# Expert 0's tokens gathered by one-hot products instead of through HBM, with second-layer biases moved ahead of the experts

## The chip, the cores and the metric

One core of a Trainium2 chip runs the whole kernel. The time is device microseconds of one execution; lower is better. All times of the trace are in microseconds from the start of the span of one profiled execution.

## The reference

One transformer block on 512 tokens of width 1024, in f32: adaptive norm, an attention mixer (sparse and block attention together, output projection `w_out`), a second norm, and a mixture of 32 experts of which each token takes 4. The part that matters here:

```python
x = x + g1 * hybrid_mixer(h, ...)                       # h @ w_out at its end
h = rms_norm(x, ln2_g) * (1.0 + sc2) + sh2
logits = h @ router_w + router_b                        # 512 x 32
top_val, top_idx = lax.top_k(logits, 4);  gate = softmax(top_val)
u = h[toks] @ w1[e] + b1[e]                             # toks: the tokens that chose e
g_, lin = u[:, :1024], u[:, 1024:]                      # clamped
y = ((lin + 1) * g_ * sigmoid(1.702 * g_)) @ w2[e] + b2[e]
x = x + g2 * segment_sum(y * gate)
```

The weights of the experts, 32 times 12.6 MB, are most of what is read.

## The kernel before

**Products.** An f32 operand is split into a high part (cast to f32r on ScalarE) and a low part (subtraction on VectorE), and a product is made of three f32r products (high-high, high-low, low-high). Each 1 MB chunk of weights, 128x2048, comes by one DMA of SyncE into one of 7 raw buffers; `high(i)` (line 770) casts it on ScalarE and `low(i)` (line 774) subtracts on VectorE, three chunks ahead of their use. The split chunks go to the pools `wq` and, from the third chunk on, `wq2`, which is opened over the memory of the closed pool `op`.

**Projection and router.** The four tiles of 128 tokens pass through `project` (lines 88 to 90 by `mm3`), four chunks of w_out each, 12 products a chunk. After the last chunk of a tile, its `tail` is cut into four steps, of which one is called behind each chunk of the next tile; those of tile 3 run at the end without products between them. `turn`: the product is added to x (`xm`, line 838), `xm` is transposed (842) and its squares summed (845), a power on GpSimd gives the norm's factor (122). `logits`: the products with the router's weights (855). `gates`: the choice of the four largest on VectorE (863 to 871), their softmax (872 to 878), the normalised rows `xs` and the gates stored to the DRAM table `h2d` (874, 879). `counts`: `xm` stored to the output (882), and five small bf16 products (899) which count, for every token and expert, the tokens ahead of it.

**Slots.** From the counts each token has a place `pos_e` in each expert, and a token that didn't choose the expert got a place behind those that did. For an expert, `slots` (1027) makes one-hot rows from the places, `lookup` (1033) turns them into token numbers by a product, and `fetch` (1036, 1002) writes them as integers and gathers these rows of `h2d` by an indirect DMA into `xg`. `none` pushes the numbers of unused slots out of range. The gather of an expert comes two experts ahead; those of experts 0 and 1 follow the router directly.

**Experts.** Each expert has 12 steps, one weight chunk each: 8 of the first layer (`pu`, 1161) and, of the expert before, 4 of the second (`py`, 1185). Into the steps are put: the transposes of the activations (`pat`, 985, in steps 1 and 2), those of the next expert's rows (`pxt`, 1009, in steps 4 and 6) with their affine part (1016) and split (1045, 1049) into `XT`, the slots, lookup and fetch two experts ahead (steps 4, 7, 9), and at step 0 `emit`: the result times gate, scattered into the output by a DMA that adds (991, 993). In experts 1 to 4 the second-layer biases of one tile are made from its gates by a transpose (787) and two products (797) and added to the output by a further DMA that adds (799).

**Order.** `in_order` ties the instructions of TensorE, VectorE and ScalarE, each engine by itself, to the order in which the code issues them, from the projection to the last expert; the DMA issues of ScalarE are among them. GpSimd and SyncE are ordered by the scheduler. A tile of a pool with two buffers may be written when the last use of the tile two before it is over, DMAs included.

Of the kernel before, what the change touches and what calls it, by code (L numbers as in the profile page):

```python
# [48 lines left out]
def block_kernel(ctx, tc, x, c, ada_w, ada_b, ln1_g, ln2_g, w_in, nsa_q_gain, nsa_k_gain, nsa_cmp_pos,  # L49
# [48 lines left out]
    G.iota(piota, pattern=[[0, 1]], base=0, channel_multiplier=1, allow_small_or_imprecise_dtypes=True)  # L98
    siota = cst.tile([P, P], F32, name="siota")
    G.iota(siota, pattern=[[1, P]], base=0, channel_multiplier=0, allow_small_or_imprecise_dtypes=True)  # L100
# [622 lines left out]
    mask = mp.tile([P, NT, NE], BF, name="mask")  # L723
    pos_e = mp.tile([P, NT, NE], F32, name="pos_e")
    tokc = mp.tile([P, NT], F16, name="tokc")
    gatef = mp.tile([P, NT, NE], F32, name="gatef")
# [5 lines left out]

    none = mp.tile([P, NE], F32, name="none")
# [44 lines left out]
    def add_b2(t, pool):  # L778

        gh = mp.tile([P, P], F32R, tag="gh", name="gh")  # L780
        gT = mp.tile([P, P], F32R, tag="gT", name="gT")

        def gates():
            pg = psm.tile([P, P], F32, tag="ps", name="pgT")
            g4 = pool.tile([P, 4, NE], F32, tag="g4", name="g4", bufs=1)
            G.tensor_copy(g4, gatef[:, t, None, :].to_broadcast([P, 4, NE]))
            T.transpose(pg, g4.rearrange("p q e -> p (q e)"), ident)
            A.copy(gh, pg)
            A.copy(gT[0:64], pg[0:64])
            V.tensor_sub(gT[64:128], pg[64:128], gh[64:128].bitcast(F32))  # L790

        def add():
            ys = pool.tile([P, D], F32, tag="ysb", name="ysb", bufs=1)
            for h in range(2):
                hs = slice(512 * h, 512 * h + 512)
                pb = psm.tile([P, 512], F32, tag="ps", name="pb2")
                T.matmul(pb, gT, b2s[:, hs], start=True, stop=True)
                A.copy(ys[:, hs], pb)
            G.dma_start(out_rows[P * t:P * t + P, :], ys, accum_op=ALU.add)

        return gates, add

    with ExitStack() as oc:
# [4 lines left out]
        onesf = op1.tile([P, NE], F32, name="onesf")  # L808
        V.memset(onesf, 1.0)
        for t in range(NT):  # L810
            V.tensor_scalar(tokc[:, t:t + 1], piota, float(P * t), None, op0=ALU.add)

        onesb = op1.tile([P, P], BF, name="onesb")
        onesn = op1.tile([P, P], BF, name="onesn")
        trib = op1.tile([P, P], BF, name="trib")
        trin = op1.tile([P, P], BF, name="trin")
        tri2 = op1.tile([P, P], BF, name="tri2")
        tileb = op1.tile([P, NT, NE], BF, name="tileb")
        V.memset(onesb, 1.0)
        V.memset(onesn, -1.0)  # L820
        for w, m in ((trib, 1.0), (trin, -1.0), (tri2, 2.0)):
            V.tensor_scalar(w, siota, piota, m, op0=ALU.is_gt, op1=ALU.mult)
        for t in range(NT):
            V.memset(tileb[:, t], float(t))

        def tail(t, ps):

            st = op.tile([P, 4], F32, tag="st2", name="st2")
            xm = op.tile([P, D], F32, tag="xm", name="xm")
            xs = op.tile([P, D], F32, tag="xs", name="xs")  # L830
            hT = op.tile([P, KD, P], F32, tag="h2T", name="h2T", bufs=1)
            lg = op.tile([P, NE + 4], F32, tag="lg", name="lg")
            g = {}

            def turn():
# [3 lines left out]
                for h in range(2):  # L839
                    pt = psc.tile([P, 4, P], F32, tag="ps", name="ph2")  # L840
                    for k in range(4):
                        T.transpose(pt[:, k, :], xm[:, 128 * (4 * h + k):128 * (4 * h + k) + 128], ident)
                    if h == 0:
                        A.copy(hT[:, 0:4, :], pt)
                        A.activation(xs, xm, AF.Square, accum_out=st[:, 0:1])
                    else:
                        V.tensor_copy(hT[:, 4:8, :], pt)
# [80 lines left out]
        for t in range(2):  # L928
            load_x(t)
# [378 lines left out]
```

## Time and profile before

| | us |
|---|---|
| median of 3 runs (lowest to highest) | 1578.86 (1577.48 to 1579.42) |
| the profiled execution | 1579.63 |
| its span, first to last instruction | 1577.9 |
| TensorE busy | 1514.2 (96%) |
| VectorE busy | 1335.3 (85%) |
| ScalarE busy | 1100.5 (70%) |
| GpSimd busy | 344.3 (22%) |

The profiled execution is 0.8 us above the median. Engines in the rows: PE is TensorE's products, PEld its weight loads (they overlap the products), DVE VectorE, ACT ScalarE, POOL GpSimd, SP SyncE; a q behind the name is the engine's queue issuing a DMA. L1161 is line 1161. A matmul's duration overlaps the next one's, so the pitch of a stream is read from starts. [...] What stands in brackets behind an instruction is the time that its engine was idle before it, and what ended it.

### The profile page before, as it was taken

What the parts mean: (1) busy time and instruction counts of PE and PEld (TensorE: products, weight loads), DVE (VectorE), ACT (ScalarE), POOL (GpSimd) and SP (SyncE); (2) the same over time, 40 slices, a digit from 0 to 9 for tenths busy, and PEclk for the clock granted to TensorE, in tenths of its full rate; (3) what the DMA queues carried; (4) which work ended last, traced back from release to release, by engine and by line L of the source; (5) the groups of instructions that cost most, each with busy time, mean ns of one, the idle gap of its engine ahead of it and who ended that gap; (6) DMA issues with size and microseconds to landing.
All of it is one profiled execution on the core that took longest, in us unless ns stands there. A gap on an engine that the chain in (4) does not pass through costs nothing.

```text
span 1577.9 us, 20500 instructions
## 1 busy us (share of the span) xinstructions
PE 1514.2 (96%) x7533; PEld 1199.3 (76%) x7533; DVE 1335.3 (85%) x1533; ACT 1100.5 (70%) x1275; POOL 344.3 (22%) x258
## 2 busy tenths in 40 slices
PE   7998999999699999999999999999999999999996
PEld 5887745457578888888888888888888888888884
DVE  4779488653689999999999999999999999999994
ACT  4332366642688887788887777778888777778872
POOL 2216445410112112111112112211111212211110
PEclk9999999999799999999999999999999999999998
DMA  9755123035699999999999999999999999999991
GB/s 327 250 203 161 55 59 106 15 120 205 265 329 356 378 368 390 371 371 373 365 372 361 371 355 370 367 367 365 369 363 371 362 361 369 379 367 364 367 366 35
DMA packets 114879, 476.04 MB, mean 302 GB/s; under 512 B 15632, under 2 KB 27984, under 8 KB 82008
## 3 DMA queue, kind: packets, MB, share of 16 engines
q1 hardware_dynamic: 102680, 449.19, 75.8%
q0 software_dynamic: 9792, 19.17, 5.3%
q10 hardware_dynamic: 2304, 6.36, 1.1%
q8 instruction: 60, 0.98, 0.2%
q14 instruction: 43, 0.35, 0.1%
HBM read 468.55 MB, written 23.13 MB: 312 GB/s over the span
## 4 chain that ended last, share of the span: by engine, by line
PE 82%; issue 6%; DMA 6%; DVE 3%; ACT 2%; POOL 1%; SPq 0%; ACTq 0%; POOLq 0%; DVEq 0%
PE pu L1161 41%; PE py L1185 19%; DMA out_dram<-ys,idx 2%; PE po L657 2%; PE pz L88 2%; PE pz L90 2%; PE pz L89 2%; PE pu L1142 2%; PE pxt L1009 2%; DMA ada<-in_ada_w_dram 2%; PE pat L985 2%; PE ps L220 2%; PE pp L636 2%; DVE am L175 1%; PE pw L89 1%
## 5 line engine op out<-in xcount | busy, mean ns | idle before, releaser
L774 DVE TENSOR_TENSOR wlo<-w,whi 128x2048 fp32r<-128x2048 f32 x384 | 868.4, 2288 | 76.7 <-ACT whi L770 76.3
L770 ACT CAST whi<-w 128x2048 fp32r<-128x2048 f32 x384 | 732.7, 1910 | 213.9 <-PE pu L1161 144.5
L1161 PE MATMUL pu<-whi,XT 128*128 128x512 f32 x2048 | 526.6, 399 | 1.4 <-ACT XT L1045 1.4
L1161 PEld LDWEIGHTS pu<-whi,XT 128*128 128x128 f32 x2048 | 374.2, 189 | 75.0 <-ACT XT L1045 1.8
L1161 PE MATMUL pu<-wlo,XT 128*128 128x512 f32 x1024 | 275.4, 391 | 0.0
L1161 PEld LDWEIGHTS pu<-wlo,XT 128*128 128x128 f32 x1024 | 192.6, 188 | 42.1
L993 POOL DMA_INDIRECT out_dram<-ys,idx x32 | 157.8, 4932 | 287.8 <-DVE ys L991 250.8
L1002 POOL DMA_INDIRECT xg<-h2d,idx x32 | 44.9, 1402 | 597.5 <-PE py L1185 537.9
L1185 PE MATMUL py<-whi,ahi 128*128 128x512 f32 x508 | 136.6, 391 | 1.0 <-DVE ys L991 0.9
L1185 PE MATMUL py<-whi,alo 128*128 128x512 f32 x508 | 135.8, 389 | 0.0
L1185 PE MATMUL py<-wlo,ahi 128*128 128x512 f32 x508 | 135.8, 389 | 0.0
L1185 PEld LDWEIGHTS py<-whi,ahi 128*128 128x128 f32 x508 | 95.0, 188 | 21.4 <-ACT ahi L1110 1.1
L1185 PEld LDWEIGHTS py<-whi,alo 128*128 128x128 f32 x508 | 95.4, 188 | 19.9
L1185 PEld LDWEIGHTS py<-wlo,ahi 128*128 128x128 f32 x508 | 95.4, 188 | 19.9
L1016 ACT ACTIVATE xf<-pxt,colv 128x128 f32<-128x128 f32 x256 | 95.9, 456 | 6.9 <-PE pxt L1009 6.9
L88 PE MATMUL pz<-whi,hhi 128*128 128x512 f32 (+2 forms) x224 | 80.9, 364 | 4.6 <-ACT hsq L422 3.6
L89 PE MATMUL pz<-wlo,hhi 128*128 128x512 f32 (+2 forms) x224 | 78.3, 352 | 0.0
L90 PE MATMUL pz<-whi,hlo 128*128 128x512 f32 (+2 forms) x224 | 77.1, 353 | 0.0
L227 ACT ACTIVATE pr<-sb,sm 128x256 f32<-128x256 f32 (+3 forms) x93 | 51.7, 557 | 24.4 <-DVE sm L224 20.7
L175 DVE SCALAR_TENSOR_TENSOR am<-ada,cond,am 128x256 f32<-128x256 f32 x128 | 61.5, 518 | 1.3 <-DMA ada<-in_ada_w_dram 0.8
L82 ACT CAST whi<-win 128x1024 fp32r<-128x1024 f32 (+3 forms) x28 | 24.2, 871 | 46.7 <-PE pz L89 21.3
L224 DVE CUSTOM_DVE_ANT_0 sb<-ps,dtile 128x128 f32<-128x128 f32 (+3 forms) x96 | 44.2, 483 | 13.9 <-PE ps L220 10.4
(287 smaller groups left out, 1617.8 us busy)
## 6 DMA issues: line engine op xcount, KB each, us to landing
w<-in_exp_w_dram SPq DMA_DIRECT2D x384, 1024.0 KB
ada<-in_ada_w_dram SPq DMA_DIRECT2D x22, 1024.0 KB
win<-in_w_in_dram SPq DMA_DIRECT2D x6, 1024.0 KB
win<-in_w_in_dram SPq DMA_DIRECT2D x3, 768.0 KB
x<-in_x_dram SPq DMA_DIRECT2D x4, 512.0 KB
ada<-in_ada_w_dram SPq DMA_DIRECT2D x4, 512.0 KB
wo<-in_w_out_dram SPq DMA_DIRECT2D x4, 512.0 KB
wo<-in_w_out_dram SPq DMA_DIRECT2D x2, 1024.0 KB
```

What stands on the lines that cost most here:

```text
L88: T.matmul(o, lhi, rhi, start=start, stop=False, **kw)
L89: T.matmul(o, lhi, rlo, start=False, stop=False, **kw)
L90: T.matmul(o, llo, rhi, start=False, stop=stop, **kw)
L175: V.scalar_tensor_tensor(am[:, p:p + MOD_W], rr[k // 4][:, c0:c0 + MOD_W], cond[:, k:k + 1], am[:, p:p + MOD_W], op0=ALU.mult, op1=ALU.add)
L227: A.activation(tl[i], sb[:, :n], AF.Exp, scale=-1.0, bias=sm[:, 0, i:i + 1], accum_out=sm[:, 1, i:i + 1])
L770: A.copy(hi, raws[i])
L774: V.tensor_sub(lo, raws.pop(i), hi.bitcast(F32))
L993: G.indirect_dma_start(out=out_rows, out_offset=bass.IndirectOffsetOnAxis(ap=icol, axis=0), in_=ys, in_offset=None, compute_op=ALU.add, bo ...
L1002: G.indirect_dma_start(out=xg, out_offset=None, in_=h2d, in_offset=bass.IndirectOffsetOnAxis(ap=icol, axis=0), bounds_check=S - 1, oob_is_ ...
L1016: A.activation(dst[:, j, :], pt[:, j, :], AF.Identity, scale=colv[:, 0, k:k + 1], bias=colv[:, 1, k:k + 1])
L1161: T.matmul(pu[h][g], XT[:, x, c, :], w[:, c0:c0 + 512], start=False, stop=last)
L1185: T.matmul(py[n], prev.a[k // 4][x][:, k % 4, :], w[:, cs], start=(k == 0 and x == 0 and w is hi), stop=(k == KD - 1 and w is lo))
```

## The change

- Expert 0 isn't gathered through `h2d`. One-hot rows of its places (`oh0`, f32, 128x128 a tile) are made behind each tile's choice, and 32 f32 products of 128x128x128 (`gather0`) add its rows up, already transposed, in two PSUM banks (`px`). The rows of all four tiles stay on chip (`rows_of`). Those of tiles 0 to 2 and the start of expert 0's bias products (`pu_start`) are issued during and after the tail of tile 3; then affine (shared by ScalarE and VectorE) and split into `XT0`. Its gates and token numbers come from an f32 lookup at step 1 of expert 0.
- Places start at 1, and a token that didn't choose an expert has place 0, so only its own tokens fill slots. `none` goes, as do three of the five counting products, their tables and the product that prepared them. Token numbers are held less 512, so that an unused slot gives 512, which is out of range.
- The second-layer bias of a tile is added to `xm` on VectorE before `xm` is stored to the output. It is called two steps after the next tile's `turn` (tile 2's between `turn` and `logits` of tile 3; tile 3's last).
- The tail's steps: `choose`, `rows`, `store`, `gates`, `place` in place of `gates` and `counts`. A chunk of tile 1 is projected before the last of tile 0, and the steps start one chunk later. x has one buffer, loaded after the tile before has been used. The squares are summed by halves.
- In each expert both transposes of the activations stand in step 1, and both of the next expert's rows in step 5 behind the lookup (then affine in steps 5 and 7, low parts in 6 and 8); slots in step 3, fetch in 7. The lookup's PSUM comes from `psc`. Expert 1's lookup and fetch stand in step 1 of expert 0, its slots before the loop. Chunk 1 is split within the end of the tail, chunk 2 after it.

The core of the diff (of lines that only moved, most are left out):

```diff
-    def add_b2(t, pool):
-        ...
-            G.dma_start(out_rows[P * t:P * t + P, :], ys, accum_op=ALU.add)
+    def affine(dst, pt, h, js=range(4)):
+        for j in js:
+            k = 4 * h + j
+            A.activation(dst[:, j, :], pt[:, j, :], AF.Identity, scale=colv[:, 0, k:k + 1], bias=colv[:, 1, k:k + 1])
+    def pu_start(e):
+        sel = [bsel[:, v, e:e + 1].to_broadcast([P, P]) for v in range(2)]
+        pu = [[psz.tile([P, 512], F32, tag="ps", name="pu") for _ in range(2)] for _ in range(2)]
+        for h in range(2):
+            for g in range(2):
+                T.matmul(pu[h][g], *bias(1024 * g + 512 * h, sel), start=True, stop=False)
+        return pu
...
+        def add_b2(t, xm):
+            gh = op1.tile([P, P], F32R, tag="gh", name="gh")
+            gT = op1.tile([P, P], F32R, tag="gT", name="gT")
+            g4 = op1.tile([P, 4, NE], F32, tag="g4", name="g4")
+            def turn():
+                G.tensor_copy(g4, gatef[:, t, None, :].to_broadcast([P, 4, NE]))
+                pg = psc.tile([P, P], F32, tag="ps", name="pgT")
+                T.transpose(pg, g4.rearrange("p q e -> p (q e)"), ident)
+                A.copy(gh, pg)
+                A.copy(gT[0:64], pg[0:64])
+                V.tensor_sub(gT[64:128], pg[64:128], gh[64:128].bitcast(F32))
+            def add():
+                for h in range(2):
+                    hs = slice(512 * h, 512 * h + 512)
+                    pb = psc.tile([P, 512], F32, tag="ps", name="pb2")
+                    T.matmul(pb, gT, b2s[:, hs], start=True, stop=True)
+                    V.tensor_add(xm[:, hs], xm[:, hs], pb)
+                nc.scalar.dma_start(out_rows[P * t:P * t + P, :], xm)
+            return turn, add
+        rows_of = [op1.tile([P, D], F32, name=f"xs{t}") for t in range(NT)]
+        def gather0(t, h, ks=range(4)):
+            for k in ks:
+                T.matmul(px[h][:, k, :], rows_of[t][:, 512 * h + P * k:512 * h + P * k + P], oh0[:, t, :], start=t == 0 and k == 0,
+                         stop=t == NT - 1 and k == 3, skip_group_check=True)
         def tail(t, ps):
             xm = op.tile([P, D], F32, tag="xm", name="xm")
-            xs = op.tile([P, D], F32, tag="xs", name="xs")
+            xs = rows_of[t]
...
+            def place():
                 m = mask[:, t, None, :]
-                count(pp[:, 0:2 + t], onesb, m.to_broadcast([P, 2 + t, NE]))
-                ...
+                T.matmul(pd[:, t], trib, mask[:, t], start=t == 0, stop=True, skip_group_check=True)
+                V.scalar_tensor_tensor(pos_e[:, t], pd[:, t], 1.0, mask[:, t], op0=ALU.add, op1=ALU.mult)
+                V.tensor_scalar(oh0[:, t], siota, pos_e[:, t, 0:1], None, op0=ALU.is_equal)
+                T.matmul(pd[:, t + 1:], onesb, m.to_broadcast([P, NT - t, NE]), start=False, stop=True,
+                         skip_group_check=True)
...
+        for t, c in [(0, 0), (0, 1), (0, 2), (1, 0), (0, 3)] + [(1, c) for c in (1, 2, 3)] + \
+                [(t, c) for t in (2, 3) for c in range(4)]:
+            if t not in ps:
+                ps[t] = [psz.tile([P, 512], F32, tag="ps", name=f"pw{t}") for _ in range(2)]
+            project(ps[t], wo[c], c, t, c == 3)
+            if todo:
+                for f in todo.pop(0):
+                    f()
+            if (t, c) == (3, 1):
+                high(0)
+                low(0)
+            if c == 3:
+                tl = tail(t, ps[t])
+                tails.append(tl)
+                if t < NT - 1:
+                    todo += [[tl.turn],
+                             [tl.logits, lambda t=t: load_x(t + 1)] + ([tails[t - 1].b2_turn] if t else []),
+                             [tl.choose, tl.rows, tl.store, tl.gates] + ([tails[t - 1].b2_add] if t else []),
+                             [tl.place]]
+        while todo:
+            for f in todo.pop(0):
+                f()
+        tl = tails[-1]
+        tl.turn()
+        tails[2].b2_turn()
+        tails[2].b2_add()
+        tl.logits()
+        px += [psc.tile([P, 4, P], F32, tag="ps", name="px") for _ in range(2)]
+        gather0(0, 0)
+        tl.choose()
+        tl.rows()
+        gather0(0, 1)
+        gather0(1, 0)
+        gather0(1, 1)
+        high(1)
+        tl.place()
+        gather0(2, 0)
+        gather0(2, 1)
+        gather0(3, 0)
+        gather0(3, 1)
+        pu0 = pu_start(0)
+        for h in range(2):
+            xf = op1.tile([P, 4, P], F32, tag="xf0", name="xf0")
+            affine(xf, px[h], h, (0, 1))
+            for j in (2, 3):
+                k = 4 * h + j
+                V.tensor_scalar(xf[:, j, :], px[h][:, j, :], colv[:, 0, k:k + 1], colv[:, 1, k:k + 1],
+                                op0=ALU.mult, op1=ALU.add)
+            A.copy(XT0[:, 0, 4 * h:4 * h + 4], xf)
+            V.tensor_sub(XT0[:, 1, 4 * h:4 * h + 4], xf, XT0[:, 0, 4 * h:4 * h + 4].bitcast(F32))
+        tl.store()
+        tl.gates()
+        low(1)
+        cnt = mp.tile([P, NE], F32, name="cnt")
+        V.tensor_copy(cnt, pd[:, NT])
+        tl.b2_turn()
+        tl.b2_add()
...
+    high(2)
+    preps[1].slots()
+    low(2)
...
-                pes[1 + h].append(turned)
+                pes[1].append(turned)
...
+        if e == 0:
+            pes[1] += [preps[1].lookup, preps[0].lookup]
+            dves[1] += [preps[1].fetch, preps[0].fetch]
+            dves[7].append(blocks_over)
         if two_on:
-            dves[4].append(two_on.slots)
-            pes[7].append(two_on.lookup)
-            dves[9].append(two_on.fetch)
+            dves[3].append(two_on.slots)
+            pes[5].append(two_on.lookup)
+            dves[7].append(two_on.fetch)
         if one_on:
             for h in range(2):
-                pes[4 + 2 * h].append(lambda h=h, p=one_on: p.turn(h))
-                acts[4 + 2 * h].append(lambda h=h, p=one_on: p.high(h))
-                dves[5 + 2 * h].append(lambda h=h, p=one_on: p.low(h))
-        if 1 <= e <= NT:
-            gates, add = add_b2(e - 1, ep)
-            pes[9].append(gates)
-            pes[11].append(add)
+                pes[5].append(lambda h=h, p=one_on: p.turn(h))
+                acts[5 + 2 * h].append(lambda h=h, p=one_on: p.high(h))
+                dves[6 + 2 * h].append(lambda h=h, p=one_on: p.low(h))
```

## Rows read from the trace of the kernel before

**Rows 1.** Stages: window, length, busy (x count) of each engine, PEclk, DMA share, GB/s.

```profile
387.90:412.90 25.00, 7.58 (x58) 5.00 (x56) 11.85 (x35) 10.46 (x16) 8.00 (x7) 0.67 0.81 297
412.90:440.46 27.56, 26.75 (x112) 20.76 (x113) 22.73 (x19) 24.66 (x27) 0.00 (x0) 0.93 0.71 270
1014.35:1050.12 35.77, 35.77 (x169) 29.38 (x168) 33.63 (x26) 28.63 (x27) 6.92 (x2) 1.00 0.99 366
```

**Rows 2.** Chain of waits across the hole: start us, us, what.

```profile
398.41 3.12 DMA out_dram<-xm
...
401.62 7.87 DMA xg<-h2d,idx
...
412.90 7.17 PE pu L1161 x22
```

**Rows 3.** Timeline, choice of experts for tile 0: start us, us, engine line op.

```profile
358.52 0.31 PE L862 MATMUL pl<-stack,ls 128*128 128x32 f32 x2
...
360.94 0.24 DVE L878 TENSOR_SCALAR gatef<-rtw,rts 128x32 f32<-128x32 f32 x1
...
361.10 1.33 DVE L838 TENSOR_TENSOR xm<-pw,xt 128x512 f32<-128x512 f32 x2
```

**Rows 4.** Timeline, weight loads of TensorE, last projection tile and a steady expert.

```profile
377.62 1.03 PEld L842 LDWEIGHTS ph<-ident,xm 128*128 128x128 f32 x8
...
378.73 0.19 PEld L89 LDWEIGHTS pw<-wol,ohi 128*128 128x128 f32 x1
...
1024.42 1.77 PEld L1161 LDWEIGHTS pu<-whi,XT 128*128 128x128 f32 x8
...
1027.14 0.59 PEld L1009 LDWEIGHTS pxt<-ident,xg 128*128 128x128 f32 x4
...
1030.34 1.77 PEld L1161 LDWEIGHTS pu<-whi,XT 128*128 128x128 f32 x8
...
1036.49 0.17 PEld L1033 LDWEIGHTS <-oh 128*128 128x128 f16 x4 [0.26 <-issue]
```

**Rows 5.** Timeline, in the hole.

```profile
388.82 1.28 DVE L838 TENSOR_TENSOR xm<-pw,xt 128x512 f32<-128x512 f32 x2
...
392.91 0.57 POOL L122 TENSOR_TENSOR st<-st,mhalf 128x1 f32<-128x1 f32 x1 [5.39 <-DVE st L121]
...
401.88 1.90 ACT L770 CAST whi<-w 128x2048 fp32r<-128x2048 f32 x1 [0.74 <-DMA out_dram<-xm]
```

**Rows 6.** Timeline, second-layer bias of tile 0 in expert 1.

```profile
467.67 0.27 ACT L788 CAST gh<-pgT 128x128 fp32r<-128x128 f32 x1 [0.85 <-PE pgT L787]
...
469.27 0.29 DVE L790 TENSOR_TENSOR gT<-pgT,gh 64x128 fp32r<-64x128 f32 x1
...
472.95 0.63 PE L797 MATMUL pb<-b2s,gT 128*128 128x512 f32 x2
```

**Rows 7.** Timeline, f32 products with 128x128 weights, two passes each.

```profile
151.02 3.52 PE L564 MATMUL psc<-kcT,qnT 128*128 128x64 f32 x16
...
294.13 1.08 PE L677 MATMUL pcr<-rw,colv 128*128 128x32 f32 x8
```

**Rows 8.** Stages, the window of the first of these (columns as in rows 1).

```profile
152.00:154.00 2.00, 2.00 (x11) 2.00 (x11) 2.00 (x3) 0.00 (x0) 2.00 (x2) 0.50 0.03 8
```

**Rows 9.** Timeline, first expert's inputs, first weight chunks.

```profile
410.69 1.50 ACT L1016 ACTIVATE xf<-pxt,colv 128x128 f32<-128x128 f32 x4 [6.92 <-PE pxt L1009]
412.23 0.62 ACT L1045 CAST XT<-xf 128x512 fp32r<-128x512 f32 x1
...
416.73 2.29 DVE L774 TENSOR_TENSOR wlo<-w,whi 128x2048 fp32r<-128x2048 f32 x1 [1.10 <-ACT whi L770]
...
417.38 1.80 PEld L1161 LDWEIGHTS pu<-whi,XT 128*128 128x128 f32 x8
```

**Rows 10.** Timeline, a gather's issue on GpSimd, expert 1.

```profile
470.02 1.23 POOL L1002 DMA_INDIRECT xg<-h2d,idx  x1 [0.64 <-DVE idx L1036]
```

**Rows 11.** Tile xg, all 32 gathers.

```profile
DMA to landing us min/median/max: 4.5/7.7/10.3
```

More of the change, by code (lines that the diff above doesn't have):

```diff
@@ L815, in block_kernel @@
         trib = op1.tile([P, P], BF, name="trib")
-        trin = op1.tile([P, P], BF, name="trin")
-        tri2 = op1.tile([P, P], BF, name="tri2")
-        tileb = op1.tile([P, NT, NE], BF, name="tileb")
         V.memset(onesb, 1.0)
[L820 to L824, printed above, removed]
+        V.tensor_scalar(trib, siota, -1.0, piota, op0=ALU.add, op1=ALU.is_gt)
@@ L833, in tail, with turn @@
             g = {}
-            def turn():
+            def turn(between=None):
+                G.memset(lg[:, NE:], NONE)
                 for h in range(2):
@@ L926, in project @@
                     parts[j][0][:, 512 * h:512 * h + 512], parts[j][1][:, 512 * h:512 * h + 512], k == 0, k == 7)
-        for t in range(2):
-            load_x(t)
-        T.matmul(po, trib, onesb, start=True, stop=False, skip_group_check=True)
-        count(po, onesb, tileb)
-        count(pd, trin, onesb)
-        count(pd, onesn, tileb)
+        load_x(0)
         load(0)
         start = len(traced())
-        steps = []
-        for t in range(NT):
-            ps = [psz.tile([P, 512], F32, tag="ps", name=f"pw{t}") for _ in range(2)]
-            for c in range(4):
-                project(ps, wo[c], c, t, c == 3)
-                if steps:
-                    steps.pop(0)()
-                    if not steps and t + 1 < NT:
-                        load_x(t + 1)
-                if t == NT - 1 and c == 1:
-                    high(0)
-                    low(0)
-            steps = list(tail(t, ps))
@@ L1010, in gather_T @@
         return pt
-    def affine(dst, pt, h):
-        for j in range(4):
-            k = 4 * h + j
-            A.activation(dst[:, j, :], pt[:, j, :], AF.Identity, scale=colv[:, 0, k:k + 1], bias=colv[:, 1, k:k + 1])
     def prep(e):
-        oh = xp.tile([P, NT, P], F16, tag="oh", name="oh", bufs=1)
         gate = xp.tile([P, 1], F32, tag="gate", name="gate", bufs=4)
         idx = xp.tile([P, 1], I32, tag="idx", name="idx", bufs=4)
-        XT = xp.tile([P, 2, KD, P], F32R, tag="XT", name="XT")
         g = {}
+        if e:
+            oh = xp.tile([P, NT, P], F16, tag="oh", name="oh", bufs=1)
+            XT = xp.tile([P, 2, KD, P], F32R, tag="XT", name="XT")
+        else:
+            oh, XT = oh0, XT0
         def slots():
@@ L1137, in block_kernel @@
             XT = me.XT
-            sel = [bsel[:, v, e:e + 1].to_broadcast([P, P]) for v in range(2)]
-            pu = [[psz.tile([P, 512], F32, tag="ps", name="pu") for _ in range(2)] for _ in range(2)]
-            for h in range(2):
-                for g in range(2):
-                    T.matmul(pu[h][g], *bias(1024 * g + 512 * h, sel), start=True, stop=False)
-            if e == 0:
-                for f in (me.turn, me.high, me.low):
-                    for h in range(2):
-                        f(h)
+            pu = pu_start(e) if e else pu0
             halves = [act_half(pu[h], ep) for h in range(2)]
```

128 lines of the change are left out of this document (52 added, 76 removed).

## The prediction

> **What bounds the kernel now.** I read the page first, then a table of busy time by stage, then the chain of waits and the timeline where that table shows a hole. On the page TensorE is the busiest engine, so only a place where it is not busy can be shortened. The table by stage [rows 1] shows that place: in a steady expert (35.77 us) TensorE is busy for all of it at full clock, in the first expert for 26.75 of 27.56 us, and in the 25.0 us between the last projection product and the first expert product for 7.58 us. The chain [rows 2] says what fills the hole: the normalised rows and the output rows must land in HBM (3.12 us), then the gather of expert 0 brings rows back (7.87 us). Some 11 of the 25 us are thus DMA, the rest is the router of the last 128 tokens. The change takes these 11 us out of the path. What counts is what it puts there.
>
> TensorE, VectorE and ScalarE issue in the order in which the code is written (`in_order`), so each instruction stands behind everything written before it on its engine. DMA issues of ScalarE stand in that order too.
>
> **1. The projection stage.** The steps of a tile now start one chunk of w_out later, and each tile's second-layer bias is added to `xm` in the step that also chooses the experts of the next tile. `xm` has two buffers: tile 2 may be written only when tile 0's rows, bias included, have been stored. From the choose product of tile 1: 2.66 us to the gates (358.52 to 361.18), 1.33 for two adds of 128x512 [rows 3], then the store, 3.12 [rows 2]: 7.1, and tile 2's first half is added by 7.8. TensorE gets there with two projection chunks (12 products each, 2.72 as in an expert, 1024.42 to 1027.14) [rows 4] and 0.9 of small products, at 6.4. It waits 1.4. The bias products and transposes moved in here cost 0.5 net of the counting products that are dropped. Together **+1.9**; 0.5 if the store lands in time, 3.4 if it takes 5 us.
>
> **2. From the last projection product to the first expert product**, now 25.0 (387.90 to 412.90) [rows 1]. I count from its start, each item behind the one before:
> - choose and gates of tile 2 on VectorE: 2.9; tile 1's bias adds 1.33: 4.2; its store lands: 7.4. Only now may tile 3's `xm` be written (it is the buffer of tile 1): 8.7. Today this add is done at 2.2 (390.10) [rows 5].
> - Transposes, two squares and the power on GpSimd: 3.2 (3.4 from the add's end to 393.48 today) [rows 5]: 11.9. Beside it ScalarE, free of the squares at 10.9, copies tile 2's gates, and the bias of tile 2 follows: 0.27 for each of two copies that overlap, then 0.29 and 0.63 [rows 6]: 12.4; adds 13.8. The copy of tile 3's logits stands on ScalarE behind the store of these rows: 14.6.
> - The gather as products: 32 products of 128x128x128 in f32, two passes each. The trace has no such product. From below, passes of 32 columns come every 0.114 us ((1.08-0.28)/7); from above, passes of 64 columns at half clock every 0.215 ((3.52-0.3)/15) [rows 7, 8]. I take 0.137, the pitch of the 128x128 f32 transposes, which have its shape (eight loads in 1.03) [rows 4]. The first 8 passes stand before the choose product of tile 3, which ends at 15.3; its mask is there at 16.7. But the next 24 passes (3.3) stand on TensorE before the placing product, so that runs at 18.7. 32 passes are left after it: 23.1, the first half at 22.2.
> - Affine, cast and low part of one half: 0.83 (two of four at 0.375 each), 0.62 [rows 9] and 0.67 [rows 3]: 24.5. The second half shares the one buffer `xf0` and repeats it: 26.8.
> - Before the first expert product TensorE has tile 3's bias products, and these wait for VectorE: gates 0.7 (the last part of the 2.66), the low part of weight chunk 1 at 2.29 [rows 9], a copy and a subtraction 0.45. With the two products: **30.9**.
>
> So the hole grows by **+5.9**. With 0.114 a pass and the store at 2.2 it is +3.7; with 0.215 it is +10.
>
> [...] The trace shows two instructions a product. [...]
>
> **3. The first expert**, now 27.56 [rows 1].
> - Its first chunk takes 4.48 (412.90 to 417.38) [rows 2, 9] where a chunk takes 2.72, since the granted clock is 0.67 over the hole [rows 1]: 1.75 us lost. TensorE now works on the one-hot products up to some 7 us before, then waits again. I give back half: -0.9 (ends -1.75 and 0).
> - Two lookups at step 1: 0.26 for the f16 one, and 8 f32 passes, 1.1: +1.4.
> - The gather of expert 1 is issued at step 1 of expert 0, and its rows are transposed at step 5. On VectorE its index stands behind the low parts of chunks 2 and 3. Chunk 2's high part goes to a buffer that lies over the old row buffers, so ScalarE waits there for the last output store, as it does now [rows 5]. From the first product: adds 1.7, store 4.85, high part 6.8, two low parts 11.4, index and GpSimd's start 12.4 (0.64 between the two) [rows 10], landing after 7.7 [rows 11]: 20.1. TensorE is there at 13.6 + 1.4 + 0.5 = 15.5: it waits **4.6** (1.4 at the shortest landing of 4.5, 7.2 at the longest of 10.3).
> Together **+5.1**, between +1.1 and +8.6.
>
> **4. Experts 1 to 4** lose the bias transposes and products: 0.13 + 0.46 [rows 4, 6], four times: **-2.4**. TensorE has no idle time there, so all of it counts.
>
> **5. Transposes in two groups, 31 experts.** Twelve products and a group of four take 3.20 us (1027.14 to 1030.34) where twelve take 2.72 [rows 4], so a group costs 0.48, four of them 1.91, and the lookup 0.26 more. Eight together and the product behind them take 1.11 (377.62 to 378.73) [rows 4], and that product takes 0.23 in a stream: 0.88. Two such groups give 0.15 an expert; but the lookup (0.26 of issue before its loads) [rows 4] now touches one of them and loses the quick start after itself, which leaves 0.065: **-2.0** over 31 (ends 0 and -4.7). ScalarE and VectorE keep their work and have three chunks of slack.
>
> "Slots for own tokens alone", the dropped tables and the tables of iota cost nothing: small VectorE work while TensorE has projection products. Without that cover they would be under 1 us.
>
> **Sum:** 1.9 + 5.9 + 5.1 - 2.4 - 2.0 = **+8.5** on the profiled execution's 1579.6 us. The median of the runs is 0.8 below it, so 1578.9 + 8.5, which I put at **1587 us**. Low ends together: 0.5 + 3.7 + 1.1 - 2.4 - 4.7 = -1.8 (1577). High ends: 3.4 + 10 + 8.6 - 2.4 = +19.6 (1598).
>
> **Rivals.**
> - *Faster: the data sets the first product, not the written order.* Place: the hole. If the row buffers, the bias of tiles 1 to 3 and the low part of chunk 1 hold nothing up, tile 3 is added at 4.2, its mask is there at 9.1, its one-hot at 9.8, the last 16 passes at 12, affine and cast at 13.5. That is -11.5 in the hole; with 0.5, +0.5 and -4.4 in the other stages, **1564 us**. For it: these 11 us of DMA do go [rows 2], and GpSimd's order is free. Against it: the other three engines follow the text. It decides faster from a first product before 19.2 us (25.0, less 2.6 for the other stages and 3.2 for the limit).
> - *No change:* the stores land early, a pass takes 0.114, expert 1's rows land in 4.5 and each expert gains 0.15, the low ends above: **1577**. For it, the landings spread widely [rows 11]; against it, the weight loads keep the DMA at 0.81 busy in the hole [rows 1].
> - *Slower still: the half clock holds through the one-hot products.* Idle TensorE is what the hole has today, and the clock falls with it [rows 1]; a pass then costs 0.215 as in a window at 0.50 [rows 7, 8]. The hole is 35.3, the first expert gets nothing back: +4.4 + 0.9, **1592**. [...]
>
> **How the numbers follow.** The forecast gets 0.47, the half clock 0.16, no change 0.15, faster 0.22. What a measurement here can tell is about 0.2%, 3.2 us. Slower takes the first two, 0.63. The likeliest case has 1582 to 1591 by itself; since faster and slower both hold much, the range for 8 in 10 goes from 1573 (a part of the fast case) to 1596.
>
> **What would show it.** In the profile after: tile 3's `xm` add waiting for the DMA of `xm`, some 7 us after the last projection product; the placing product right behind 24 gather passes; the first expert product behind the bias products of tile 3 and over 28 us after the last projection product; expert 0 waiting for `xg` at its step 5; experts 1 to 4 at the steady period; that period at 35.6 to 35.75. I am wrong if the first product comes before 22 us, if `xg` is there in time and the period falls by 0.3, or if `xm` waits for no DMA.

## The result, and the profile after

The changed kernel takes 1602.84 us (median of 4 runs, 1600.84 to 1607.76), the kernel before 1579.14 beside it: a ratio of 1.0154, 95% interval 1.0127 to 1.0180. It is slower, as forecast, but by 23.7 us where 8.5 were forecast. The profiled execution took 1600.84 us, its span is 1599.1 (before 1577.9), so 21.2 us are to be found in the trace. The windows below end where the forecast's parts end; they answer to [rows 1].

Stages of the changed kernel: what was added to the projection stage, the hole up to tile 3's sum, from there to the first expert product, the first expert, a steady expert. Columns as in [rows 1], the busy times in the order PE, PEld, DVE, ACT, POOL; PEclk is the clock granted to TensorE, 1.00 being the full one.

```profile
387.90:392.81 4.91, 4.91 (x37) 3.59 (x35) 2.59 (x2) 2.59 (x5) 0.10 (x1) 1.00 0.48 162
392.81:404.54 11.73, 1.45 (x8) 0.80 (x6) 3.14 (x14) 0.32 (x1) 0.64 (x3) 0.71 0.86 338
404.54:431.86 27.32, 16.53 (x102) 13.82 (x103) 11.45 (x30) 8.71 (x19) 5.06 (x6) 0.69 0.15 54
431.86:468.78 36.92, 30.16 (x125) 23.83 (x123) 26.84 (x30) 23.77 (x23) 5.27 (x2) 0.86 0.72 278
1038.59:1074.18 35.59, 35.59 (x170) 29.47 (x169) 33.64 (x26) 28.51 (x27) 8.33 (x2) 1.00 0.99 366
```

| part | forecast | measured |
|---|---|---|
| projection stage | +1.9 | +4.9 |
| hole, 25.0 before | +5.9 | +14.0 (39.05) |
| first expert, 27.56 before | +5.1 | +9.4 |
| the other experts | -4.4 | -7.1 |
| sum | +8.5 | +21.2 |

The two lines with the largest excess, the projection stage and the hole, share one mechanism. Timeline of the changed kernel around the sums of tiles 2 and 3 (start us, us, engine line op; in brackets what ended the idle time before):

```profile
376.20 17.13 SPq L66 DMA_DIRECT2D w<-in_exp_w_dram  x5
376.67 0.34 ACTq L836 DMA_DIRECT2D out_dram<-xm  x1
383.29 1.29 DVE L867 TENSOR_TENSOR xm<-pw,xt 128x512 f32<-128x512 f32 x2 [6.23 <-DMA out_dram<-xm]
...
396.94 0.34 ACTq L836 DMA_DIRECT2D out_dram<-xm  x1
404.54 1.29 DVE L867 TENSOR_TENSOR xm<-pw,xt 128x512 f32<-128x512 f32 x2 [7.21 <-DMA out_dram<-xm]
405.29 1.97 PE L872 MATMUL ph<-ident,xm 128*128 128x128 f32 x8 [8.04 <-DVE xm L867]
```

The stores of tiles 0 and 1 are issued at 376.67 and 396.94, and the sums that need their buffers start 6.6 and 7.6 us later. I had put 3.12 from [rows 2] between issue and sum. The weight loads on SP's queue (first line) run beside both stores: the DMA share in stages of 2 us is 0.59 to 1.06 from 376 to 384 and 0.98 to 1.02 from 396 to 402. Stages of 2 us of the changed kernel, whose second store left at 396.94:

```profile
398.00:400.00 2.00, 0.00 (x0) 0.00 (x0) 0.00 (x0) 0.00 (x0) 0.00 (x0) 0.50 1.02 416
...
402.00:404.00 2.00, 0.00 (x0) 0.00 (x0) 0.00 (x0) 0.00 (x0) 0.00 (x0) 0.50 0.56 224
404.00:406.00 2.00, 0.71 (x4) 0.72 (x5) 1.29 (x2) 0.00 (x0) 0.00 (x0) 0.50 0.00 0
```

And of the kernel before, whose store of [rows 2] left at 398.41:

```profile
398.00:400.00 2.00, 0.47 (x9) 0.41 (x9) 1.34 (x3) 0.76 (x1) 0.00 (x0) 0.50 0.93 358
400.00:402.00 2.00, 1.97 (x6) 1.05 (x4) 1.77 (x8) 1.26 (x2) 0.38 (x1) 0.50 0.54 218
402.00:404.00 2.00, 0.00 (x0) 0.00 (x0) 1.60 (x2) 1.78 (x1) 2.00 (x1) 0.50 0.00 0
```

The second number from the right is the DMA share. Both of these stores are done when the loads run out, near 404 and 401.5; the old one was issued close to the end of its burst, the new one 1.5 us earlier in a burst that lasts 2 us longer. The changed kernel's first store left only 0.5 us after its burst began (376.20) and was done by 383.29, while the loads ran on to about 385 (DMA share 1.06 from 382 to 384, 0.41 from 384 to 386). So a store needn't wait for the end of a burst, and how its time hangs on its place in one is not shown. The second store has ScalarE's own load of x (390.25) and row store (392.13) ahead of it on its queue; whether they are part of its 7.6 us is not shown. Ahead of the first the DMA was nearly idle (share 0.05 from 374 to 376), and it took 6.6 all the same.

Behind the second wait TensorE's eight transposes take 1.97 us at a granted clock of 0.50 (404 to 408); in [rows 4] eight loads of them took 1.03, at 1.00 (376 to 380).

The third line is the written order. The end of the hole in the changed kernel:

```profile
421.98 0.62 ACT L1007 CAST XT<-xf 128x512 fp32r<-128x512 f32 x1 [0.85 <-DVE xf L1005]
422.63 0.69 DVE L1008 TENSOR_TENSOR XT<-xf,XT 128x512 fp32r<-128x512 f32 x1 [0.74 <-ACT XT L1007]
...
426.91 2.29 DVE L779 TENSOR_TENSOR wlo<-w,whi 128x2048 fp32r<-128x2048 f32 x1
427.07 2.18 POOL L913 COPY tok<-gatef 128x1 f32<-128x1 f32 x1 [10.97 <-DVE gatef L911]
429.19 0.29 POOL L823 COPY g<-gatef 128x128 f32<-128x128 f32 x1
429.53 0.48 PE L825 MATMUL pgT<-ident,g 128*128 128x128 f32 x1 [7.42 <-POOL g L823]
...
430.84 1.22 PE L834 MATMUL pb<-b2s,gT 128*128 128x512 f32 x2 [0.84 <-DVE gT L828]
...
431.86 3.62 PE L1214 MATMUL pu<-whi,XT 128*128 128x512 f32 x8
```

The first half of the first expert's inputs is cast at 422.60 and has its low part at 423.32, and chunk 0 could start. TensorE stands at tile 3's gate transpose instead, and its products come 9.3 us after the cast. The half clock shows in the last line too: eight products in 3.62 us, at a granted clock of 0.52 over them (431.86 to 435.48).

In the first expert TensorE waits for the gathered rows of expert 1, as forecast:

```profile
443.46 2.50 POOL L1062 DMA_INDIRECT xg<-h2d,idx  x1 [13.99 <-ACT whi L775]
453.28 1.97 PE L1069 MATMUL pxt<-ident,xg 128*128 128x128 f32 x8 [4.52 <-DMA xg<-h2d,idx]
```

At the first expert's end stands a wait that no forecast had: for ScalarE's `sg`, ahead of the next expert's bias products. The changed kernel, the kernel before, and e2 below, which has only the regrouped transposes:

```profile
467.73 1.44 PE L795 MATMUL pu<-biasr,bsel 128*128 128x512 f32 x4 [2.24 <-ACT sg L1032]
```

```profile
438.73 2.12 PE L1142 MATMUL pu<-biasr,bsel 128*128 128x512 f32 x4 [0.68 <-ACT sg L972]
```

```profile
441.57 1.89 PE L1142 MATMUL pu<-biasr,bsel 128*128 128x512 f32 x4 [2.34 <-ACT sg L972]
```

It is 1.6 us longer and comes with the regrouping: in both kernels that have it, ScalarE makes expert 1's affine part and cast (2.1 us together) between its last weight cast and `sg`, and in the kernel before it made them ahead of that weight cast.

### The profile page after: what moved, and what is told of

The parts are those of the page before. It is cut to its first block, busy times and chain, and to the rows that moved or that the text cites. A ratio compares the mean times of both kernels' runs of the same rounds, so it can differ in the third digit from the quotient of the medians.

```text
span 1599.1 us, 20609 instructions
## 1 busy us (share of the span) xinstructions
PE 1520.1 (95%) x7578; PEld 1214.5 (76%) x7578; DVE 1341.8 (84%) x1549; ACT 1092.7 (68%) x1271; POOL 391.5 (24%) x257
## 4 chain that ended last, share of the span: by engine, by line
PE 64%; issue 5%; DMA 3%; ACT 1%; DVE 0%; POOL 0%; POOLq 0%; ACTq 0%; DVEq 0%
PE pu L1214 39%; PE py L1238 19%; DMA out_dram<-ys,idx 2%; PE pxt L1069 2%; PE pu L795 2%; PE pat L1045 2%; DMA xg<-h2d,idx 1%; ACT whi L775 0%; DMA out_dram<-xm 0%; PE pi L1091 0%; DVE wlo L779 0%; ACT xf L787 0%; ACT L1032 0%; DVE xm L835 0%; POOL out_dram L1053 0%
## 5 line engine op out<-in xcount | busy, mean ns | idle before, releaser
L1214 PE MATMUL pu<-whi,XT 128*128 128x512 f32 x2048 | 518.6, 396 | 0.0
L1214 PEld LDWEIGHTS pu<-whi,XT 128*128 128x128 f32 x2048 | 383.0, 190 | 78.6
L1053 POOL DMA_INDIRECT out_dram<-ys,idx x32 | 170.6, 5331 | 431.0 <-DVE ys L1051 431.0
L1062 POOL DMA_INDIRECT xg<-h2d,idx x31 | 84.8, 2735 | 471.4 <-issue 424.3
L1238 PEld LDWEIGHTS py<-whi,ahi 128*128 128x128 f32 x508 | 95.3, 188 | 21.2 <-ACT ahi L1170 1.1
L787 ACT ACTIVATE xf<-pxt,colv 128x128 f32<-128x128 f32 x248 | 92.6, 453 | 4.8 <-PE pxt L1069 4.8
L88 PEld LDWEIGHTS pz<-whi,hhi 128*128 128x128 f32 x224 | 42.5, 191 | 14.2 <-ACT hsq L423 5.6
```

The lines of the kernel that those rows point to most:

```text
L88: T.matmul(o, lhi, rhi, start=start, stop=False, **kw)
L787: A.activation(dst[:, j, :], pt[:, j, :], AF.Identity, scale=colv[:, 0, k:k + 1], bias=colv[:, 1, k:k + 1])
L1053: G.indirect_dma_start(out=out_rows, out_offset=bass.IndirectOffsetOnAxis(ap=icol, axis=0), in_=ys, in_offset=None, compute_op=ALU.add, bo ...
L1062: G.indirect_dma_start(out=xg, out_offset=None, in_=h2d, in_offset=bass.IndirectOffsetOnAxis(ap=icol, axis=0), bounds_check=S - 1, oob_is_ ...
L1214: T.matmul(pu[h][g], XT[:, x, c, :], w[:, c0:c0 + 512], start=False, stop=last)
L1238: T.matmul(py[n], prev.a[k // 4][x][:, k % 4, :], w[:, cs], start=(k == 0 and x == 0 and w is hi), stop=(k == KD - 1 and w is lo))
```

## The experiments

Each ratio is to the kernel before on the same chip in the same session; "less" is against the changed kernel, the difference of the two ratios times 1579 us, where nothing else is said. By the 95% intervals of the two ratios such a difference is uncertain by some 4 to 6 us. Theory: two late stores and tile 3's bias products ahead of the first expert product make up the loss. Rivals: the one-hot route, or the half clock.

**e1: the stores' buffers.**

```diff
-            xm = op.tile([P, D], F32, tag="xm", name="xm")
+            xm = xts[t]
...
-            xts.append(op1.tile([P, D], F32, tag="xt2", name="xt2"))
+            xts.append(op1.tile([P, D], F32, tag="xm", name="xm", bufs=3))
```

> The changed kernel with the row x + attention of each tile summed in place into its x tile, three buffers in rotation instead of two xm and one x. Theory (the store of tile t-2 landing late beside the weight loads is the cost): tile 2's and tile 3's sums no longer wait, so the last projection product ends near 388 instead of 392.8 (-4 us) and tile 3's sum stands 1 us behind it instead of 11.7 (-10), with 1 to 3 us more back from the clock: 1585 to 1589 us against 1602.8. Rival (the written order of the tail sets the hole: second-layer bias of tile 2 and 24 one-hot passes ahead of what the first expert needs): the wait only covers that order, and 5 to 8 us come back: 1595 to 1598. Rival (the clock falls at each wait whatever its length): under 3 us beyond the stage's 4.

1589.39 us, ratio 1.0065 (1.0053 to 1.0078): 14.1 less, at the edge of the theory's 1585 to 1589 and far from the rival's 1595 to 1598. The two waits were 13.4 together. Its trace around the sum of tile 3 and the first product:

```profile
397.39 1.29 DVE L867 TENSOR_TENSOR xm<-pw,xm 128x512 f32<-128x512 f32 x2 [1.95 <-DMA xm<-in_x_dram]
398.14 1.97 PE L872 MATMUL ph<-ident,xm 128*128 128x128 f32 x8 [2.75 <-DVE xm L867]
...
425.06 1.48 PE L1214 MATMUL pu<-whi,XT 128*128 128x512 f32 x3
```

The sum waits no longer for a store, but 1.95 us for x of tile 3, a load that the change issues later. From this sum to the first product it is 27.7 us, as before the repair (27.3): the wait was on the path whole. No clock came back: the eight transposes take 1.97 us again, though TensorE waited 2.75 us and not 8.04, and the granted clock is 0.74 from 390 to 400 and 0.58 from 400 to 410.

**e11: are the stores late because of the weight loads?**

```diff
+        if held:
+            V.memset(r[:, 0:1], 0.0)
...
-        load(0)
...
+        held.append(1)
+        load(0)
+        held.clear()
```

> The changed kernel with the weight loads of the experts held back until tile 3's sum is done (a one-column memset on VectorE goes ahead of each of the first seven loads; the split of chunk 0 moves behind the choice of tile 3). Theory (the stores of xm land late because 1 MB weight loads fill the DMA): both stores land in 3 to 3.5 us, tile 2's sum no longer waits, tile 3's waits 2.5 to 3 instead of 7.2: 8 to 9 us less, 1594; some of it lost if chunks 0 and 1 are then late. Rival (these stores take 7 us by themselves, or their wait hides another): the two waits stay and the time is 1602 or more.

1593.35 us, ratio 1.0089 (1.0067 to 1.0110): 10.3 less. What VectorE waited for ahead of work on `xm` between 370 and 435 us (us, times), in the changed kernel and then in e11:

```profile
  DMA out_dram<-xm: 13.4, 2
```

```profile
  DMA out_dram<-xm: 4.6, 2
```

And its timeline:

```profile
374.80 0.34 ACTq L840 DMA_DIRECT2D out_dram<-xm  x1
...
377.45 1.29 DVE L871 TENSOR_TENSOR xm<-pw,xt 128x512 f32<-128x512 f32 x2 [2.26 <-DMA out_dram<-xm]
...
389.61 0.34 ACTq L840 DMA_DIRECT2D out_dram<-xm  x1
...
392.34 1.29 DVE L871 TENSOR_TENSOR xm<-pw,xt 128x512 f32<-128x512 f32 x2 [2.35 <-DMA out_dram<-xm]
```

With no loads beside them (DMA share 0.34, the store's own, from 374 to 378 and from 389 to 393) the same stores let the sums start 2.65 and 2.73 us after their issue, not 6.6 and 7.6. That the loads make the stores late is shown by this run: chunk 0's split, which moved with the loads, and the one-column clears ahead of the seven held loads are the only other changes. Tile 2's sum, which I expected to wait no more, still waits 2.26 us. Beside the running loads, in the changed kernel, the times from issue to sum are 2.5 and 2.8 times as long.

**e6: the written order.** Tile 3's bias leaves the hole, for an accumulating store in expert 1 as before.

```diff
-            b2 = add_b2(t, xm)
+            b2 = add_b2(t, xm) if not last else (None, None)
...
+                if last:
+                    nc.scalar.dma_start(out_rows[P * t:P * t + P, :], xm)
...
-        tl.b2_turn()
-        tl.b2_add()
...
+        if e == 1:
+            b2g, b2a = acc_b2(NT - 1, ep)
```

> The changed kernel with the bias of tile 3 alone left out of the hole: it goes back to an accumulating store in expert 1; tiles 0 to 2 stay as changed, with their waits. Theory (written order: the first expert product stands on TensorE behind tile 3's bias products, 9.3 us after its data are there): the first product comes 9 us earlier after tile 3's sum (18 us instead of 27.3). Of that, 3 to 4 us are lost again in step 1, where the lookups then wait for VectorE (4.0 in the kernel with all biases undone), and 0.6 in expert 1: 1596 to 1598 us against 1602.8. Rival (nothing given back): 1592 to 1594. Rival (the hole's length is the half clock's and the stores' alone): 1601 to 1603.

1590.89 us, ratio 1.0078 (1.0066 to 1.0090): 12.0 less.

```profile
406.04 1.29 DVE L892 TENSOR_TENSOR xm<-pw,xt 128x512 f32<-128x512 f32 x2 [7.42 <-DMA out_dram<-xm]
...
424.04 2.13 PE L1243 MATMUL pu<-whi,XT 128*128 128x512 f32 x8 [0.55 <-ACT XT L1034]
...
431.61 0.25 PE L1116 MATMUL pi<-tokc,oh 128*128 128x1 f16 x4 [4.51 <-ACT whi L775]
...
446.63 1.09 PE L1094 MATMUL pxt<-ident,xg 128*128 128x128 f32 x8 [0.27 <-DMA xg<-h2d,idx]
```

The store's wait is as it was, and 18.0 us after the sum the first product follows its own data. The lookups in step 1 wait 4.51 us as expected, yet that is not an extra loss: the wait for `xg` shrinks from 4.52 to 0.27. The loss in the first expert only changed its place. The rival "nothing given back" (1592 to 1594) comes closest, and the run lies 1 us below its low end.

**e7: e1 and e6 together.** The edits are those above.

> Both repairs together: the sum in place in three buffers, and tile 3's bias by accumulating store. If waits and order are separate costs they add: 1589.4 less what the repair of tile 3 gives alone (4 to 9 us): 1581 to 1585. If the clock ties them together, more: 1577 to 1580. What is left over the kernel with all biases undone (1579.5) is then the bias of tile 2 ahead of the logits, 3 to 5 us, less 1.9 that three experts no longer pay.

1577.84 us, ratio 0.9991 (0.9978 to 1.0003): 25.7 less, where e1 and e6 alone give 26.1. The two costs add within the noise, and together they are as large as the whole net loss (24.3 by the ratio): the interval holds 1.

**e3: all biases undone.**

```diff
+                nc.scalar.dma_start(out_rows[P * t:P * t + P, :], xm)
...
-        tails[2].b2_turn()
-        tails[2].b2_add()
...
-        tl.b2_turn()
-        tl.b2_add()
...
+        if 1 <= e <= NT:
+            b2g, b2a = add_b2(e - 1, ep)
```

> The changed kernel with one part undone: the second-layer biases go back to accumulating stores in experts 1 to 4, and xm is stored from the placing step of its own tile. Theory (late stores behind the added biases): the stage gets 4 back, the hole 9 to 12, high part 2's wait for the last store goes too (1 to 2), experts 1 to 4 pay 0.7 each: 1588 to 1592. Rival (the one-hot route is the cost): 4 back from the stage, 2.7 paid: 1600 to 1602.

1579.46 us, ratio 0.9999 (0.9986 to 1.0012): 24.5 less, more than I expected, since I had not yet seen that tile 3's products held the first one up. It also uncovers the late load of x, and shows the price of a bias in an expert (second expert with one, then a steady expert):

```profile
395.93 1.29 DVE L866 TENSOR_TENSOR xm<-pw,xt 128x512 f32<-128x512 f32 x2 [3.89 <-DMA xt<-in_x_dram]
```

```profile
482.09:518.33 36.24, 36.24 (x173) 29.89 (x172) 34.12 (x26) 29.69 (x31) 5.60 (x4) 1.00 1.01 373
1053.20:1088.76 35.56, 35.56 (x170) 29.46 (x169) 33.63 (x26) 28.50 (x27) 8.33 (x2) 1.00 0.98 375
```

An accumulating bias costs its expert 0.68 us (forecast 0.59).

**e5: the one-hot route undone.** Expert 0 is gathered through DRAM as before; the biases stay on chip.

```diff
-        gather0(0, 0)
...
+    for e in range(2):
+        preps[e].slots()
+        preps[e].lookup()
+        preps[e].fetch()
...
+            if e == 0:
+                for f in (me.turn, me.high, me.low):
+                    for h in range(2):
+                        f(h)
```

> The changed kernel with the other part undone: the first expert's inputs come by gather through DRAM as before, biases still added on chip. Theory (late stores): the stage and the 11.7 us from the last product to tile 3's sum stay; the hole stays at 36 to 38; the first expert loses the late gather of expert 1 and the half clock in its first chunk, 5 to 8 us: 1594 to 1599. Rival (the one-hot route is the cost): 15 to 20 us come back, 1582 to 1587.

1593.22 us, ratio 1.0089 (1.0076 to 1.0102): 10.3 less, a little more than the theory's 4 to 9 and far from the rival's 16 to 21. Beside the biases the one-hot route is itself a loss here: in e5, without it, the stretch from the last projection product to the first expert product takes 37.4 us against 39.05, and the first expert, without the late gather of expert 1, takes 28.1 us up to the next expert's first bias load against 35.9.

**e2: the regrouped transposes alone, on the kernel before.**

```diff
-                pes[1 + h].append(turned)
+                pes[1].append(turned)
...
-            dves[4].append(two_on.slots)
-            pes[7].append(two_on.lookup)
-            dves[9].append(two_on.fetch)
+            dves[3].append(two_on.slots)
+            pes[5].append(two_on.lookup)
+            dves[7].append(two_on.fetch)
...
-                pes[4 + 2 * h].append(lambda h=h, p=one_on: p.turn(h))
+                pes[5].append(lambda h=h, p=one_on: p.turn(h))
```

> The kernel before with one part of the change: both transposes of the activations in step 1, lookup and both transposes of the inputs in step 5, slots in step 3, fetch in step 7. Theory: the steady period falls from 35.77 to 35.59, 31 times: -5.6 us, 1573.5. Rival (my forecast of the part): -2.0, 1577; the rest of the experts' -7.1 then belongs to the accumulating bias stores that are gone from experts 1 to 4. Rival: no gain without the other parts.

1576.13 us, ratio 0.9979 (0.9967 to 0.9991): 3.3 below the kernel before. Its steady expert takes 35.53 us, 0.24 less than in [rows 1], more than either expectation; over 31 experts that would be 7.4. Part is lost at the start, where the first expert takes 27.5 us up to the next one's first bias load and before took 25.8; that is the longer wait for `sg`, 2.34 us instead of 0.68:

```profile
414.10:441.57 27.47, 25.14 (x108) 20.24 (x109) 22.57 (x18) 22.99 (x26) 2.70 (x1) 0.92 0.70 269
1050.11:1085.64 35.53, 35.53 (x170) 29.46 (x168) 33.63 (x26) 28.52 (x27) 8.29 (x2) 1.00 0.99 370
```

**e10: the half clock alone.**

```diff
+                T.matmul(dp, ohi[:, 0, 0:P], wo[0][0][0][:, 0:512], start=True, stop=True)
...
+        warm(28, psz)
         tl.turn()
+        warm(3, psz)
...
+        warm(30, psc)
```

> The changed kernel with products added whose result nobody reads, only to keep TensorE busy where it waits: 28 ahead of tile 3's transposes, 3 behind them, 30 between the bias products of expert 0 and those of tile 3. No wait and no order is changed. It prices the half clock alone. From the rows of the changed kernel, half clock costs 0.9 in the transposes, 0.5 in the bias products, 0.4 in the logits, 0.8 and 0.7 in the first 32 one-hot passes and 1.7 in the first chunk: theory (these lie on the path): 4 to 5 us less, 1598 us. Rival (the tail is set by the other engines, only the chunk gains): 1.5 to 2, 1601. Rival (the half clock is the main cost): 10 us or more, 1593.

1600.23 us, ratio 1.0128 (1.0100 to 1.0156), 4.1 less: its interval overlaps that of the changed kernel, so the gain is not settled. The trace tells more:

```profile
406.86 1.29 DVE L867 TENSOR_TENSOR xm<-pw,xt 128x512 f32<-128x512 f32 x2 [7.18 <-DMA out_dram<-xm]
407.61 1.25 PE L872 MATMUL ph<-ident,xm 128*128 128x128 f32 x8
...
422.28 0.69 DVE L1016 TENSOR_TENSOR XT<-xf,XT 128x512 fp32r<-128x512 f32 x1 [0.74 <-ACT XT L1015]
...
430.98 2.02 PE L1223 MATMUL pu<-whi,XT 128*128 128x512 f32 x8
...
453.30 1.97 PE L1078 MATMUL pxt<-ident,xg 128*128 128x128 f32 x8 [5.89 <-DMA xg<-h2d,idx]
```

At full clock (granted 1.00 from 404 to 436) it is 24.1 us from the sum to the first product, 3.2 less, and chunk 0's first eight products take 2.02 instead of 3.62. But TensorE then waits 5.9 us for `xg` instead of 4.5, so what the clock gives to chunk 0 is taken back by the gather. The half clock is worth some 3 us here; it is not the main cost.

**e8, e9, e12: towards a kernel that beats both.** e8 is e3 with x summed in place in three buffers and loaded early; e9 puts expert 1's slots and gather ahead; e12 moves one low part.

```diff
+        for t in range(3):
+            load_x(t)
...
+        tl.store()
+        tl.gates()
+        V.tensor_tensor(oh1, siota[:, None, :].to_broadcast([P, NT, P]),
...
+    preps[1].lookup()
+    preps[1].fetch()
```

> The kernel with all biases undone, and now x summed in place in three buffers, so that x of tile 3 is loaded a whole tile earlier. Theory (the single x buffer of the changed kernel is one more late DMA, covered by the wait for the store so far: 3.9 us of VectorE's wait, the load landing after 9 us): tile 3's sum stands 1 us behind the last product, 3 to 4 us come back: 1575 to 1577 us; 1573 if the clock then holds through the logits. Rival (the load lands late wherever it is, or another wait takes over): 1579.

1575.83 us, ratio 0.9975 (0.9963 to 0.9988): 3.8 below e3, as the theory had it.

> The kernel just before, with the first expert's order changed: the store and gates of tile 3 and the slots of expert 1 right behind the placing product, its index and gather ahead of the first chunk, low parts of chunks 1 and 2 behind them, lookups of expert 0 in step 2. Theory (in the first expert the one-hot route loses 4.0 us in step 1 to lookups that wait for VectorE, 4.5 at step 5 to the late gather of expert 1, and 1 to 2 to the clock after these waits): 8 to 10 us less than the kernel just before: 1566 to 1568, below both kernels. Rival (the gather lands late because of the weight loads, however early it is issued, or low part 1 is now late): 2 to 4 us less: 1572 to 1574.

1572.47 us, ratio 0.9963 (0.9948 to 0.9977): 3.4 below e8 by the medians of one session, at the rival's end, but 1.9 by the ratios, whose intervals overlap: the gain over e8 is not settled. `xg` is in time (its transposes wait for no DMA), but low part 1 is now late:

```profile
414.19 1.20 PE L1218 MATMUL pu<-wlo,XT 128*128 128x512 f32 x4 [1.38 <-DVE wlo L780]
```

> The kernel e9 with low part 1 moved up by one place, to VectorE's idle time while the last 32 one-hot passes run (it held chunk 1 up by 1.8 us, and the chunk behind ran at half clock, 1.4 us more). Theory: 2.5 to 3.5 us less: 1569. Rival (low part 1 then delays the affine of the first expert's inputs by as much): 1572.

1569.70 us, ratio 0.9950 (0.9925 to 0.9976): about 2 us below e9 by the ratios, within both intervals and so not settled; 7.9 us (0.5%) below the kernel before and 32 below the changed one. Its first expert runs at full clock throughout:

```profile
409.40:436.69 27.29, 24.65 (x117) 19.74 (x117) 23.75 (x27) 23.95 (x25) 2.48 (x2) 1.00 0.79 302
```

## Why the prediction was wrong

The direction and each place of loss were as forecast; the sizes were not.

- **The step that failed is the landing of the stores.** The forecast put "3.12" twice into its sums, for tile 0's store in part 1 and tile 1's in part 2, and took the wait in the projection stage for 1.4 us. Both stores run beside the weight loads and hold their buffers for 6.6 and 7.6 us. In the projection stage TensorE waits 4.2 us instead of 1.4, 2.8 of the 3.0 by which the stage exceeds its forecast, and the second store moves tile 3's sum from the forecast 7.4 us behind the last product to 11.7. e1 and e11 show that these waits are 10 to 14 us of the time. My high end, "if it takes 5 us", was too low as well (and by the terms beside it 5 us make 3.8, not 3.4; in the hole's sum, in the same way, the terms give 24.3 where I wrote 24.5). The row's 3.12 was right for a store near the end of a burst of loads, and I carried it to stores issued earlier in one without a look at the DMA share beside it.
- **From tile 3's sum on** the forecast had 30.9 - 7.4 = 23.5 us. The trace has 27.3, and 24.1 in e10, where the clock is held up. So 3.2 us are the half clock, which I carried as a rival with 0.16 and put at nothing in the sum. It doesn't come from the late stores: in e1 the sum waits for no store, and the eight transposes behind it take the same 1.97 us, and the stretch is as long (27.7). That the rest comes near the forecast is partly luck: up to the first half's low part I had 17.1 (7.4 to 24.5) and e10 has 16.1 (406.86 to 422.97), from there to the first product I had 6.4 and e10 has 8.0.
- **Tile 3's bias ahead of the first product** was in the forecast, 24.5 to 30.9 or 6.4 us behind the first half's low part. It is 8.5 (423.32 to 431.86): tile 3's gates start 3.0 us behind this low part (426.33) where I had 2.3, and GpSimd's copy of 0.2 us takes 2.18, so that the gates' copy for the transpose ends at 429.48. e6 gives the price of the whole step, 12.0.
- **The one-hot passes.** The 32 products are 64 passes, two each. In the changed kernel the last 32 come every 0.114 us (granted clock 1.00 from 416 to 422) and the first 8 every 0.22, at half clock (0.50 from 410 to 414); I took 0.137 for all. A product is thus 0.23 us at full clock and 0.44 at half, where I had 0.27.
- **The first expert.** The wait for `xg` was forecast as 4.6 and is 4.52, by luck: counted from the first product the rows are there at 21.4 where I had 20.1, since the landing takes 9.8 us and not 7.7, and TensorE arrives at 16.9 where I had 15.5. Chunk 0 gets no clock back (3.62 us for eight products, -0.9 forecast). Behind the wait for `xg` the granted clock is 0.55 and 0.60 (452 to 460), and 0.68 as expert 1 starts (468 to 472). The eight products behind the wait take 3.76 us where eight at full clock take 2.02 (from 459.75; granted 1.00 from 460 to 462), and the next four 1.45 instead of 1.09: some 2 us. The wait for `sg` adds 1.6. The forecast had no term for these two; with the 0.9 of chunk 0 they come to about the 4.3 us that it lacks.
- **The experts.** The regrouping was forecast as 0.065 us an expert; the changed kernel's steady expert is 0.18 shorter, e2's 0.24. This error was to the good, and some 3 us.
- **Rivals.** "The data sets the first product" fell: 25.7 us come back once the two orders that hold it up are taken out. "The half clock holds" came about in part, at 3.2 us in the hole and the 0.9 of chunk 0, and not as a consequence of the stores.

What stays open: how much of e2's steady gain is the grouping of the transposes and how much the moved lookup, and some 0.6 us of the 2.3 by which e5's first expert (28.1) exceeds the 25.8 before: 1.65 are the wait for `sg` (2.33 us in e5).

## What to carry to other kernels

A store that frees a buffer is a wait for whoever writes that buffer next: take its length from a row with the same load beside it (here 2.7 us without weight loads, 6.6 and 7.6 beside them), and ask for one more buffer, or for a sum in place, before moving work ahead of the store. Where engines issue in written order, work that nothing needs soon (here an output bias) must not stand between a stage's data and its first product, however short it is by itself. Two such costs of 14 and 12 us added up here, and undoing them turned a loss of 1.5% into a draw.

## What the runs showed of the hardware

- A 512 KB store let the sum that waited for it start 2.65 and 2.73 us after its issue with no weight loads beside it (e11), and 6.6 and 7.6 us after it beside 1 MB loads on another queue (the changed kernel); the x load of the same size, issued at 386.21 in e3, let its sum start 9.7 us later.
- GpSimd's copy of 128x1 took 0.19 us while VectorE added a bias from PSUM to one SBUF operand (the lines below, the changed kernel) and 2.18 while VectorE ran a subtraction of two SBUF operands (the lines of 426.91 and 427.07 above). It took 2.18 in e1 (420.27) and e10 (426.72) as well, each time beside this subtraction (420.11 and 426.57). What holds the copy up is not shown.

```profile
395.63 1.28 DVE L835 TENSOR_TENSOR xm<-xm,pb 128x512 f32<-128x512 f32 x2
395.78 0.19 POOL L913 COPY tok<-gatef 128x1 f32<-128x1 f32 x1 [1.52 <-DVE gatef L911]
```

- Products whose result nobody reads brought TensorE's granted clock back to 1.00 before a wait of 7 us was over: in e10, whose sum waits until 406.86, it is 0.80 from 400 to 408 and 1.00 from 404 to 408, thus 0.60 from 400 to 404, and the eight transposes behind the wait take 1.25 us instead of the changed kernel's 1.97. In time this helped only as far as the next wait.
